# A vector spread over the partitions by TensorE instead of by a DMA, and one column of the first modulation made by sixteen one-column matmuls

## The chip, the cores and the metric

One core of a Trainium2 chip. Its engines each run their own instructions in order and wait for each other by semaphores: TensorE (PE; PEld is its weight load), VectorE (DVE), ScalarE (ACT), GpSimd (POOL) and SyncE (SP), which here issues all DMAs. The metric is device time in microseconds, median of several runs. Times below count from the start of the profiled span.

## The reference

Two layers on x of 256 tokens by 2048 channels, all float32. Layer 0 is a Mamba-2 mixer, layer 1 a dilated window attention. Each layer modulates its input by a conditioning vector c, and only this matters here:

```
shift, scale, gate = split(silu(c) @ ada_w[layer] + ada_b[layer], 3)
h = x * (1.0 + scale) + shift
proj = h @ a_in_w            # layer 0: 2048 -> 10304 columns
```

So shift and scale of layer 0, 2048 numbers each, must be there before the first big product starts, 128 channels (one tile kt of 16) at a time.

## The kernel before

**Big products.** Activations lie channel by token (tile kt is 128 channels by 256 tokens). Every float32 operand of a big product is split into a high part (a copy on ScalarE, rounded to the float32r type) and a low part (a subtraction on VectorE), and three float32r matmuls make one product. A weight "piece" is 128 x 1024 floats, 0.52 MB, and holds two tiles kt by 512 columns. It comes by DMA into `raw` (6 buffers, `load_piece`, L87-90), is split by `split` (L92-99) into `whi` (L95, ScalarE) and `wlo` (L97, VectorE), 4 buffers each, and is used either by `cm_piece` (24 matmuls of 256 columns, L121-123) or by `tm_piece` (12 matmuls of 512 columns, L169-171).

**The modulation.** silu(c) lies in `cb_`, the same 2048 numbers on every partition: a DMA that reads c 128 times (`bcast`, L67) and a SiLU on ScalarE (L68). A column (128 values of shift or scale) is made by `ada_load` (a DMA of 1.05 MB, `araw<-in_ada`, L240) and `ada_dot` (one VectorE multiply with running sum over 128 x 2048, L247). `ada_bias` (L252) adds the bias row. Then `h_step` (L381-400) makes tile kt of h: htmp (L397, ScalarE), its high part actT (L398, ScalarE) and its low part (L399, VectorE).

**Stage one**, up to about 180 us, interleaves the 32 columns of layer 0 with the pieces. A hand-written list, `order`, gives the order of the pieces; its first entries are z/B/C pieces b4:0, b6:0, h (first piece of B/C group 0), z2:0, b2:0, x1:0. In front of the loop stand the first DMAs, all on SP's queue: c, columns scale 0 and shift 0, x, the bias, pieces 0 and 1, scale 1, piece 2. Each `h_step` fetches another column, and each turn of the loop one more piece, so that five pieces are fetched ahead of the one in use. PE works on a tile kt as soon as its h is there. A scheduler places each engine's instructions in order of its own estimate, so that a change in one place can move instructions in another.

**Stage two**, from about 180 us, computes dt and the scan of each head group: `stage1` (seg, L567-570; xd and the like, L580-588, VectorE) and `stage2` (py, L608, PE, float32; po, L600), with the remaining pieces in between. L351 and L358 add a stored part of a product to its rest.

Of the kernel before, what the change touches and what calls it, by code (L numbers as in the profile page):

```python
# [9 lines left out]
F32 = mybir.dt.float32  # L10
F32R = mybir.dt.float32r
I32 = mybir.dt.int32
AF = mybir.ActivationFunctionType
ALU = mybir.AluOpType
# [4 lines left out]
P = 128  # L19
L = 256  # L20
D = 2048
KT = D // P
# [24 lines left out]


@with_exitstack
def trunk(ctx, tc, xT, x, c, par, cst, bias, lnrow, ada, wdt, win, wout, wk, wv, wbin, wbout, out):  # L50
    nc = tc.nc
    V, S, T, PO = nc.vector, nc.scalar, nc.tensor, nc.gpsimd

    cons = ctx.enter_context(tc.tile_pool(name="cons", bufs=1))
    wp = ctx.enter_context(tc.tile_pool(name="wp", bufs=3))
# [3 lines left out]
    mm = ctx.enter_context(tc.tile_pool(name="mm", bufs=4, space=PSUM))  # L59
    aux = None  # L60

    def bcast(dst, src, off=0):
        nc.sync.dma_start(dst, bass.AP(tensor=src.tensor, offset=src.offset + off,
                                       ap=[[0, P], [1, dst.shape[-1]]]))

    cb_ = cons.tile([P, D], F32, name="cb_")
    bcast(cb_, c)  # L67
    S.activation(cb_, cb_, AF.Silu)  # L68
    NB = OFF["adab"][1]
    adab_ = cons.tile([P, NB], F32, name="adab")  # L70
    prm = cons.tile([P, NPAR - NB], F32, name="prm")
    cc = cons.tile([P, NCONST], F32, name="cc")

    cons.tile([P, 32], F32, name="pad")

    def pv(name):
        a, b = OFF[name]
# [4 lines left out]
    cbmask = cc[:, CM:CM + 384]  # L82
    ones = cons.tile([P, P], F32, name="ones")
    V.memset(ones, 1.0)


    def load_piece(src):  # L87
# [86 lines left out]
    def tm_pair():  # L174
        return [mm.tile([P, 512], F32, name="acc") for _ in range(2)]
# [52 lines left out]
    mod = [cons.tile([P, KT, 3], F32, name=f"mod{i}") for i in range(2)]  # L228
# [3 lines left out]
    def shift(i, kt):  # L232
        return mod[i][:, kt, 0:1]

    def scale(i, kt):
        return mod[i][:, kt, 1:2]

    def ada_load(pool, layer, kind, ct):
        raw = pool.tile([P, D], F32, name="araw", bufs=2)
        nc.sync.dma_start(raw, ada[layer, KIND.index(kind), ct])  # L240
        return raw

    def ada_dot(layer, kind, ct, raw):

        j = KIND.index(kind)
        with tc.issue_after(pin[0]) if pin[0] is not None else ExitStack():
            V.scalar_tensor_tensor(raw, raw, 1.0, cb_, op0=ALU.mult, op1=ALU.mult,  # L247
                                   accum_out=mod[layer][:, ct, j:j + 1])

    def ada_bias(layer, kts, kinds):  # L250
        m = mod[layer][:, kts, kinds]
        V.tensor_tensor(m, m, adab[:, layer, kts, kinds], op=ALU.add)  # L252
# [33 lines left out]
    with ExitStack() as cA:  # L286
# [14 lines left out]
        with ExitStack() as cS:  # L301
            wp1 = cS.enter_context(tc.tile_pool(name="wp1", bufs=2))
# [62 lines left out]
            with ExitStack() as c0:  # L365
# [1 line left out]
                ex = c0.enter_context(tc.tile_pool(name="ex", bufs=4, space=PSUM))  # L367
                first = [acc_pair(ex), acc_pair(ex)]
                cols = [(0, kind, kt) for kt in range(KT) for kind in ("scale", "shift")]
                raws, xts, late = [], {}, []  # L370

                def fetch():
                    i = len(raws)
                    if i < len(cols):
                        raws.append(ada_load((wp1, pe)[i // 2 % 2], *cols[i]))

                def fetch_x(kt):
                    xts[kt // 2] = pe.tile([P, 2, L], F32, name="xt")
                    nc.sync.dma_start(xts[kt // 2], xT[:, kt:kt + 2, :])

                def h_step():  # L381

                    _, kind, kt = cols[h_step.i]
                    raw = raws[h_step.i]
                    h_step.i += 1
                    if kind == "scale" and kt % 2 == 0 and kt:
                        fetch_x(kt)
                    ada_dot(0, kind, kt, raw)
                    if kt > 1:
                        pin[0] = None  # L390
                    fetch()
                    while late:
                        late.pop()()
                    if kind == "shift":
                        ada_bias(0, slice(kt, kt + 1), slice(0, 2))
                        t = pe.tile([P, L], F32, name="htmp")
                        S.activation(t, xts[kt // 2][:, kt % 2, :], AF.Identity, bias=shift(0, kt), scale=scale(0, kt))  # L397
                        S.activation(hhi[:, kt, :], t, AF.Copy)  # L398
                        late.append(lambda: V.tensor_tensor(hlo[:, kt, :], t, hhi[:, kt, :].bitcast(F32),  # L399
                                                            op=ALU.subtract))  # L400
# [7 lines left out]
                for row in ("b4:0. b6:0. h z2:0. b2:0 x1:0 h", "b2:1. x1:1. z1:0 z1:1. z4:0 h h",  # L408
# [3 lines left out]
                    for w in row.split():  # L412
                        if w == two:
                            n = -2 if sum(o[0] == -2 for o in order) == sum(o[0] == -1 for o in order) else -1
# [6 lines left out]
                pieces = []  # L421

                def fetch_piece():
                    if len(pieces) < len(order):
                        k, q, _ = order[len(pieces)]
                        pieces.append(load_piece(source[k][q]))

                fetch()
                fetch()
                fetch_x(0)  # L430
                nc.sync.dma_start(adab_, par[:, :NB])
                V.tensor_scalar(adab[:, :, :, 1:3], adab[:, :, :, 1:3], 1.0, None, op0=ALU.add)
                fetch_piece()
                fetch_piece()
                fetch()
                fetch_piece()
                for _ in range(2):
                    for _ in range(2):
                        h_step()
                    while late:  # L440
                        pin[0] = late.pop()().ins
                    fetch_piece()

                def dt_piece(q, raw):
# [26 lines left out]
                            else:  # L471
                                S.activation(place, ps[w], AF.Copy)

                begin, done, ended, halves = {}, set(), [], {}
                for i, (k, q, ends) in enumerate(order):
                    fetch_piece()
                    if i == 16:
# [236 lines left out]
        for n in range(4):  # L714
            ps = tm_chunk(wout[n], lambda kt: yhi[kt // 16][:, kt % 16, :], lambda kt: ylo[kt // 4][:, kt % 4, :],
                          nk=2 * KT, rate=(1, 4) if n else (0, 1),
                          pre={0: y_ahead, 3: first_weights}.get(n), split_end=4 if n == 3 else 0)
# [45 lines left out]
    with ExitStack() as cL:  # L763
# [25 lines left out]
        with tc.issue_after(tile4.ins):  # L789
# [12 lines left out]
            late = latest[-1].ins  # L802
# [123 lines left out]
    for n in range(2):  # L926
        ps = tm_chunk(wbout[n], *og, nk=H)
# [12 lines left out]
    ps = [tm_pair() for _ in range(2)]  # L940
# [19 lines left out]
    halves = [ps[1], [None, aux2.tile([P, 512], F32, name="po")]]  # L960
# [31 lines left out]
def _cm(v):  # L992

    return v.reshape(-1, P).T
# [9 lines left out]
def _dt(w):  # L1004

    a = np.zeros((2, 8, P, P), w.dtype)
    a[..., :64] = w.reshape(2, 8, P, 64)
    return a.transpose(0, 2, 1, 3).reshape(2, P, 1024)


def _layout(x, c, ada_w, ada_b, ln_g, ln_b, a_in_w, a_conv_w, a_conv_b, a_dt_bias,
            a_A_log, a_D, a_norm_g, a_out_w, kv_w, b_in_w, b_out_w):
    f = np.float32
    par = np.zeros((P, NPAR), f)

    def put(name, a):
        par[:a.shape[0], OFF[name][0]:OFF[name][1]] = a

    ab = ada_b.reshape(2, 3, KT, P)
    put("adab", ab.transpose(3, 0, 2, 1).reshape(P, 96))  # L1020
    put("convw", a_conv_w[0].T.reshape(48, P, 4).transpose(1, 0, 2).reshape(P, 192))
    put("convb", _cm(a_conv_b[0]))
    put("normg", _cm(a_norm_g[0]))
    put("dsk", np.broadcast_to(a_D[0], (P, 64)))
    put("dtb", a_dt_bias[0][:, None])
    put("alog", np.broadcast_to(a_A_log[0], (P, 64)))
    put("lng", _cm(ln_g[0]))
    put("lnb", _cm(ln_b[0]))

    cst = np.zeros((P, NCONST), f)  # L1030
    i = np.arange(P)
    cst[:, CI:CI + 128] = np.eye(P)
    up = (i[:, None] <= i[None, :]).astype(f)
    cst[:, CT:CT + 128] = up
    cst[:, CM:CM + 384] = np.concatenate([up, up, np.ones((P, P), f)], 1)
    bias = np.zeros((P, NBIAS), f)
    delta = 128 + i[:, None] - np.arange(256)[None, :]
    bias[:, CD:CD + 256] = -delta
    for g, (win_, dil) in enumerate(((128, 1), (512, 4), (2048, 16))):
        ok = (delta >= 0) & (delta % dil == 0) & (delta <= win_)  # L1040
        bias[:, CA + 256 * g:CA + 256 * g + 256] = np.where(ok, 0.0, NEG)


    ada = ada_w.reshape(2, D, 3, KT, P).transpose(0, 2, 3, 4, 1)

    w = a_in_w[0]
    z, xs, bb, cc, dt = (w[:, a:b] for a, b in ((0, 4096), (4096, 8192), (8192, 9216), (9216, 10240), (10240, 10304)))
    bc = np.stack([bb.reshape(D, G, P), cc.reshape(D, G, P)], 2).reshape(D, 2048)
    win = _pieces(np.concatenate([bc, xs, z], 1))
    return {  # L1050
        "xT": x[0].T.reshape(KT, P, L).transpose(1, 0, 2), "x": x[0], "c": c, "par": par, "cst": cst, "bias": bias,
        "lnrow": np.stack([ln_g[0], ln_b[0], ln_g[1], ln_b[1]]),
        "ada": ada, "wdt": _dt(dt), "win": win,
        "wout": _pieces(a_out_w[0]), "wk": _pieces(kv_w[:, :3072], 256, 4),
        "wv": _pieces(kv_w[:, 3072:]), "wbin": _pieces(b_in_w[0], 256, 4), "wbout": _pieces(b_out_w[0]),
    }
# [20 lines left out]
```

## Time and profile before

| | |
|---|---|
| median of 3 runs | 1275.31 us (1274.89 to 1276.96) |
| profiled execution, device time | 1274.67 us |
| its span in the trace | 1272.5 us |
| PE busy | 1236.6 us, 97% |
| DVE busy | 1034.5 us, 81% |
| ACT busy | 704.0 us, 55% |
| DMA queue q1 | 334.69 MB, 73.5% of 16 engines' span |
| first matmul | 15.01 us |

A row of the timeline gives start, duration, engine, source line, operation, the tile written and read, and in brackets the idle time ahead of it with what ended it. "L" numbers are lines of the kernel before, unless a row is said to be of the changed kernel, whose lines are some 26 (around the splits) to 41 (in stage two) higher.

### The profile page before, as it was taken

The numbers are of one execution on the slowest core, as the hardware profiler recorded it, in microseconds if no ns is written. First come the engines' busy times: TensorE is split into PE (matmuls) and PEld (weight loads), VectorE is DVE, ScalarE is ACT, GpSimd is POOL, SyncE is SP. The second block draws the span as 40 slices with busy tenths as digits, with TensorE's granted clock in tenths as the row PEclk, the third lists the DMA queues.
The fourth block names the chain that finished last, engine by engine and source line by source line (L and its number), as shares of the span: only waits on it lengthen the run. The fifth ranks groups of instructions, "written<-read, shape, count | busy, mean of one in ns | idle before, by whom it ended". The sixth has DMA issues, their size and how long they took to land.

```text
span 1272.5 us, 19056 instructions
## 1 busy us (share of the span) xinstructions
PE 1236.6 (97%) x7222; PEld 1078.7 (85%) x7222; DVE 1034.5 (81%) x1498; ACT 704.0 (55%) x1035; POOL 0.2 (0%) x4
## 2 busy tenths in 40 slices
PE   4999999999999999999999999999999999999997
PEld 4889989899898999778888788888878888888885
DVE  6999986999998878869776678878888867758876
ACT  3655577757677777764344445434345645444731
POOL 0000000000000000000000000000000000000000
PEclk9999999999999999999999999999999999999999
DMA  9999968696866546468988469989998774463751
GB/s 386 423 420 422 420 211 298 224 341 234 314 247 208 157 149 216 167 216 292 338 282 282 160 195 353 357 328 348 357 381 316 235 240 130 127 204 100 222 192 66
DMA packets 80588, 335.89 MB, mean 264 GB/s; under 512 B 9105, under 2 KB 9329, under 8 KB 67697
## 3 DMA queue, kind: packets, MB, share of 16 engines
q1 hardware_dynamic: 80496, 334.69, 73.5%
q8 instruction: 56, 0.92, 0.3%
q14 instruction: 36, 0.29, 0.1%
HBM read 332.47 MB, written 2.18 MB: 263 GB/s over the span
## 4 chain that ended last, share of the span: by engine, by line
PE 85%; DVE 8%; DMA 3%; issue 2%; ACT 1%; SPq 0%; DVEq 0%; ACTq 0%
PE acc L145 14%; PE acc L171 12%; PE acc L170 12%; PE acc L169 12%; PE acc L148 7%; PE acc L123 7%; PE acc L121 7%; PE acc L122 7%; DVE araw L247 2%; DVE wlo L97 2%; PE py L608 2%; PE aux L850 1%; DMA araw<-in_ada 1%; DMA raw<-in_wk 1%; PE po L873 1%
## 5 line engine op out<-in xcount | busy, mean ns | idle before, releaser
L95 ACT ACTIVATE whi<-raw 128x1024 fp32r<-128x1024 f32 x392 | 411.3, 1058 | 369.4 <-PE acc L171 127.3
L97 DVE TENSOR_TENSOR wlo<-raw,whi 128x1024 fp32r<-128x1024 f32 x392 | 473.3, 1220 | 140.3 <-ACT whi L95 139.5
L145 PE MATMUL acc<-actT,whi 128*128 128x512 f32 x896 | 285.9, 398 | 0.0
L170 PE MATMUL acc<-wlo,actT 128*128 128x512 f32 x688 | 269.7, 392 | 1.1 <-DVE wlo L97 0.9
L169 PE MATMUL acc<-whi,actT 128*128 128x512 f32 x688 | 266.7, 394 | 0.9 <-ACT actT L663 0.9
L121 PE MATMUL acc<-actT,whi 128*128 128x256 f32 x768 | 217.4, 285 | 17.5 <-ACT actT L398 17.3
L247 DVE SCALAR_TENSOR_TENSOR araw<-araw,cb__72 128x2048 f32<-128x2048 f32 x96 | 219.2, 2284 | 14.6 <-DMA araw<-in_ada 14.5
L123 PE MATMUL acc<-actT,wlo 128*128 128x256 f32 x768 | 214.9, 285 | 4.9 <-DVE wlo L97 4.9
L122 PE MATMUL acc<-actT,whi 128*128 128x256 f32 x768 | 217.1, 284 | 0.0
L148 PEld LDWEIGHTS acc<-actT,wlo 128*128 128x128 f32 x896 | 167.0, 188 | 42.1 <-DVE wlo L97 5.0
L148 PE MATMUL acc<-actT,wlo 128*128 128x256 f32 x896 | 180.9, 282 | 1.9 <-DVE wlo L97 1.2
L171 PE MATMUL acc<-whi,actT 128*128 128x512 f32 x432 | 168.7, 391 | 0.0
L121 PEld LDWEIGHTS acc<-actT,whi 128*128 128x128 f32 x768 | 147.7, 193 | 18.7 <-ACT actT L398 17.5
L170 PEld LDWEIGHTS acc<-wlo,actT 128*128 128x128 f32 x688 | 129.3, 188 | 29.1 <-DVE wlo L97 3.4
L123 PEld LDWEIGHTS acc<-actT,wlo 128*128 128x128 f32 x768 | 146.5, 193 | 6.0 <-DVE wlo L97 5.8
L169 PEld LDWEIGHTS acc<-whi,actT 128*128 128x128 f32 x688 | 128.7, 188 | 26.7 <-ACT actT L663 1.4
L122 PEld LDWEIGHTS acc<-actT,whi 128*128 128x128 f32 x768 | 148.1, 193 | 0.3
L145 PEld LDWEIGHTS acc<-actT,whi 128*128 128x128 f32 x896 | 137.5, 189 | 0.3
L171 PE MATMUL acc<-whi,ylo 128*128 128x512 f32 x256 | 100.5, 393 | 0.0
L171 PEld LDWEIGHTS acc<-whi,actT 128*128 128x128 f32 x432 | 81.1, 188 | 16.6
L171 PEld LDWEIGHTS acc<-whi,ylo 128*128 128x128 f32 x256 | 48.0, 188 | 9.7
L319 DVE SCALAR_TENSOR_TENSOR cacc<-acc,prm,cacc 128x253 f32<-128x253 f32 (+2 forms) x96 | 42.1, 474 | 6.1 <-ACT cacc L316 5.8
(251 smaller groups left out, 1110.2 us busy)
## 6 DMA issues: line engine op xcount, KB each, us to landing
araw<-in_ada SPq DMA_DIRECT2D x96, 1024.0 KB, 7.5
raw<-in_win SPq DMA_DIRECT2D x160, 512.0 KB, 5.6
raw<-in_wout SPq DMA_DIRECT2D x64, 512.0 KB, 4.8
raw<-in_wbin SPq DMA_DIRECT2D x64, 512.0 KB, 4.3
raw<-in_wv SPq DMA_DIRECT2D x48, 512.0 KB, 5.4
raw<-in_wk SPq DMA_DIRECT2D x48, 512.0 KB, 7.7
cbc<-cumd SPq DMA_DIRECT2D x16, 512.0 KB, 5.2
raw<-in_wbout SPq DMA_DIRECT2D x16, 512.0 KB, 4.7
```

The costliest lines, as they stand in the source:

```text
L95: copied.append(S.activation(hi, raw, AF.Copy))
L97: latest.append(V.tensor_tensor(lo, raw, hi.bitcast(F32), op=ALU.subtract))
L121: T.matmul(o, hi[:, k, c_], ahi[:, kt, :], start=first, stop=False, skip_group_check=True)
L122: T.matmul(o, hi[:, k, c_], alo[:, kt, :], start=False, stop=False, skip_group_check=True)
L123: T.matmul(o, lo[:, k, c_], ahi[:, kt, :], start=False, stop=kt == k1 - 1, skip_group_check=True)
L145: T.matmul(ps[n], hi[:, k, n * P:n * P + P], xp[:, kt], start=kt == 0, stop=False, skip_group_check=True)
L148: T.matmul(ps[n][:, 0, :], lo[:, k, n * P:n * P + P], xhi[:, kt, :], start=False, stop=kt == KT - 1, skip_group_check=True)
L169: T.matmul(o, h_, hi[:, k, :], start=kt == k0, stop=False, skip_group_check=part)
L170: T.matmul(o, h_, lo[:, k, :], start=False, stop=False, skip_group_check=part)
L171: end = T.matmul(o, l_, hi[:, k, :], start=False, stop=kt == k1 - 1, skip_group_check=part)
L247: V.scalar_tensor_tensor(raw, raw, 1.0, cb_, op0=ALU.mult, op1=ALU.mult, accum_out=mod[layer][:, ct, j:j + 1])
L319: V.scalar_tensor_tensor(acc[:, o:], ps[:, :L - o], w[:, j:j + 1], acc[:, o:], op0=ALU.mult, op1=ALU.add)
```

## The change

1. **c.** The DMA of c into all partitions goes. The host now lays c out as 128 x 528: columns 0 to 511 hold the four quarters of c, quarter j on partitions 32j to 32j+31, and columns 512 to 527 hold c by rows (channel 128k+p at partition p, column k). `spread_c` loads it, applies SiLU, keeps the last 16 columns as `ccol`, splits the 512 others into high and low, and multiplies them by 0/1 matrices `pick` (made by GpSimd memsets) in eight matmuls of 512 columns. Four PSUM banks are copied to `cb_`, two by ScalarE, two by VectorE.
2. **First shift column.** Fetch number 1 loads `adak` (the same 1.05 MB of weights, laid out so that channels stand on the partitions). Its dot product on VectorE becomes sixteen float32 matmuls with one moving column each (`raw` block k as weights, `ccol[:, k]` moving), and a copy of 128 values from PSUM.
3. **Order at the start.** Piece 0 is split ahead of the first `h_step`, piece 1 after the first tile, and one `fetch_piece` less stands ahead of the loop, so that four pieces are fetched ahead instead of five.

```diff
-    bcast(cb_, c)
-    S.activation(cb_, cb_, AF.Silu)
+    def spread_c():
+        cq = wp.tile([P, 1024], F32, name="raw", bufs=6)[:, :512 + KT]
+        nc.sync.dma_start(cq, c)
+        pick = wp.tile([P, 1024], F32R, name="whi", bufs=4)[:, :512].rearrange("p (j m) -> p j m", j=4)
+        PO.memset(pick.bitcast(F32), 0.0)
+        for j in range(4):
+            PO.memset(pick[32 * j:32 * j + 1, j, :].bitcast(F32), 1.0)
+        S.activation(cq, cq, AF.Silu)
+        V.tensor_copy(ccol, cq[:, 512:])
+        half = wp.tile([P, 1024], F32R, name="wlo", bufs=4).rearrange("p (i n) -> p i n", i=2)
+        S.activation(half[:, 0, :], cq[:, :512], AF.Copy)
+        V.tensor_tensor(half[:, 1, :], cq[:, :512], half[:, 0, :].bitcast(F32), op=ALU.subtract)
+        ps = [mm.tile([P, 512], F32, name="acc") for _ in range(4)]
+        for js in ((0, 1), (2,), (3,)):
+            for i in range(2):
+                for j in js:
+                    T.matmul(ps[j], pick[:, j, :], half[:, i, :], start=i == 0, stop=i == 1)
+        for j in range(4):
+            d = cb_[:, 512 * j:512 * j + 512]
+            if j % 2:
+                V.tensor_copy(d, ps[j])
+            else:
+                S.activation(d, ps[j], AF.Copy)
...
                 def fetch():
                     i = len(raws)
-                    if i < len(cols):
+                    if i == 1:
+                        raws.append(wp1.tile([P, D], F32, name="araw", bufs=2))
+                        nc.sync.dma_start(raws[1], adak)
+                    elif i < len(cols):
...
-                    ada_dot(0, kind, kt, raw)
+                    if h_step.i == 2:
+                        pm = mm.tile([P, 2, L], F32, name="acc")[:, 0, 0:1]
+                        for k in range(KT):
+                            T.matmul(pm, raw[:, k * P:k * P + P], ccol[:, k:k + 1], start=k == 0, stop=k == KT - 1)
+                        with tc.issue_after(dot[0]):
+                            V.tensor_copy(mod[0][:, 0, 0:1], pm)
+                    else:
+                        dot[0] = ada_dot(0, kind, kt, raw).ins
...
+                halves = {}
+                spread_c()
                 fetch()
                 fetch()
                 fetch_x(0)
...
                 fetch_piece()
-                fetch_piece()
                 fetch()
                 fetch_piece()
-                for _ in range(2):
-                    for _ in range(2):
-                        h_step()
+                halves[0] = split(pieces[0])
+                for i in range(2):
+                    h_step()
+                    h_step()
                     while late:
                         pin[0] = late.pop()().ins
+                    if i == 0:
+                        halves[1] = split(pieces[1])
                     fetch_piece()
```

**At the start, on VectorE.** Below is the head of VectorE's program, after two memsets: before, then changed. `mod` holds the columns, `araw` the weights of a column, `adab` the bias.

```order
L247 SCALAR_TENSOR_TENSOR araw,mod_84<-araw,cb__72 128x2048 x2
L432 TENSOR_SCALAR adab<-adab 128x32x2
L252 TENSOR_TENSOR mod_84<-mod_84,adab 128x2
L97 TENSOR_TENSOR wlo<-raw,whi 128x1024
L399 TENSOR_TENSOR actT<-htmp,actT 128x256
L97 TENSOR_TENSOR wlo<-raw,whi 128x1024
L247 SCALAR_TENSOR_TENSOR araw,mod_84<-araw,cb__72 128x2048
L97 TENSOR_TENSOR wlo<-raw,whi 128x1024
L247 SCALAR_TENSOR_TENSOR araw,mod_84<-araw,cb__72 128x2048
L252 TENSOR_TENSOR mod_84<-mod_84,adab 128x2
```

```order
L107 COPY cb__72<-acc_141 128x512 [waits PE_49]
L273 SCALAR_TENSOR_TENSOR araw_154,mod0_83<-araw_154,cb__72 128x2048 [waits DMAHW1_49,DVE_49,Activation_49]
L471 TENSOR_SCALAR adab_73<-adab_73 128x32x2 [waits DMAHW4_49]
L423 COPY mod0_83<-acc_175 128x1 [waits PE_49]
L278 TENSOR_TENSOR mod0_83<-mod0_83,adab_73 128x2 [waits DVE_49]
L123 TENSOR_TENSOR wlo_169<-raw_162,whi_168 128x1024 [waits DMAHW5_49,Activation_49]
L436 TENSOR_TENSOR actT_87<-htmp_196,actT_87 128x256 [waits Activation_49]
L273 SCALAR_TENSOR_TENSOR araw_164,mod0_83<-araw_164,cb__72 128x2048 [waits DMAHW6_49]
L123 TENSOR_TENSOR wlo_201<-raw_166,whi_200 128x1024 [waits DMAHW7_49,Activation_49]
L273 SCALAR_TENSOR_TENSOR araw_173,mod0_83<-araw_173,cb__72 128x2048 [waits DMAHW0_49]
L278 TENSOR_TENSOR mod0_83<-mod0_83,adab_73 128x2 [waits DVE_49]
```

The second dot (L247) became a copy that waits for PE (L423), and two splits of pieces instead of three stand ahead of the second bias.

**In stage two, on VectorE**, around the first head group (`s` is y of the group, `xd` its input times dt): before, then changed.

```order
L97 TENSOR_TENSOR wlo<-raw,whi 128x1024 x6
L358 TENSOR_TENSOR s_95<-acc,s_95 128x512 x2
L557 TENSOR_TENSOR cb<-aux,cc 128x384
...
L580 TENSOR_TENSOR xd<-aux,dtT 128x512
L583 TENSOR_TENSOR s_95<-aux,prm 128x512
L97 TENSOR_TENSOR wlo<-raw,whi 128x1024 x3
L601 TENSOR_TENSOR xo<-aux,dec 128x512
```

```order
L123 TENSOR_TENSOR wlo<-raw,whi 128x1024 x5
L384 TENSOR_TENSOR s_94<-acc,s_94 128x512 x2
L598 TENSOR_TENSOR cb<-aux,cc 128x384
...
L621 TENSOR_TENSOR xd<-aux,dtT 128x512
L624 TENSOR_TENSOR s_94<-aux,prm 128x512
L123 TENSOR_TENSOR wlo<-raw,whi 128x1024 x4
L642 TENSOR_TENSOR xo<-aux,dec 128x512
```

One split of a piece moved from ahead of the group to behind it.

**In stage two, on PE**, at the same group (`py` is its product, `acc` a big product): before, then changed.

```order
L169 MATMUL acc<-whi,actT 128x512 x2
L608 MATMUL py<-xd,seg 128x64 x8
L121 MATMUL acc<-actT,whi 128x256
L600 MATMUL aux<-xo,cb 128x512
L608 MATMUL py<-xd,seg 128x64 x8
L122 MATMUL acc<-actT,whi 128x256
```

```order
L195 MATMUL acc<-whi,actT 128x512 x2
L649 MATMUL py<-xd,seg 128x64 x8
L641 MATMUL aux<-xo,cb 128x512
L649 MATMUL py<-xd,seg 128x64 x8
L595 MATMUL aux<-bcm 128x2x128
L596 MATMUL aux<-bcm 128x128
```

Between the transposes ahead of them (L578, changed L619) and the first py, PE has 32 matmuls of 512 columns before and 20 in the changed kernel; the other 12, one piece, come behind the py.

More of the change, by code (lines that the diff above doesn't have):

```diff
@@ L49, in trunk @@
 @with_exitstack
-def trunk(ctx, tc, xT, x, c, par, cst, bias, lnrow, ada, wdt, win, wout, wk, wv, wbin, wbout, out):
+def trunk(ctx, tc, xT, x, c, par, cst, bias, lnrow, ada, adak, wdt, win, wout, wk, wv, wbin, wbout, out):
     nc = tc.nc
@@ L72, in trunk @@
     cc = cons.tile([P, NCONST], F32, name="cc")
-    cons.tile([P, 32], F32, name="pad")
+    cons.tile([P, 16], F32, name="pad")
     def pv(name):
@@ L84, in trunk @@
     V.memset(ones, 1.0)
+    ccol = cons.tile([P, KT], F32, name="ccol")
+    def spread_c():
[21 more added lines that the diff above has]
+                S.activation(d, ps[j], AF.Copy)
     def load_piece(src):
@@ L246, in ada_dot @@
         with tc.issue_after(pin[0]) if pin[0] is not None else ExitStack():
-            V.scalar_tensor_tensor(raw, raw, 1.0, cb_, op0=ALU.mult, op1=ALU.mult,
-                                   accum_out=mod[layer][:, ct, j:j + 1])
+            return V.scalar_tensor_tensor(raw, raw, 1.0, cb_, op0=ALU.mult, op1=ALU.mult,
+                                          accum_out=mod[layer][:, ct, j:j + 1])
     def ada_bias(layer, kts, kinds):
@@ L369, in trunk @@
                 cols = [(0, kind, kt) for kt in range(KT) for kind in ("scale", "shift")]
-                raws, xts, late = [], {}, []
+                raws, xts, late, dot = [], {}, [], [None]
                 def fetch():
                     i = len(raws)
-                    if i < len(cols):
+                    if i == 1:
+                        raws.append(wp1.tile([P, D], F32, name="araw", bufs=2))
+                        nc.sync.dma_start(raws[1], adak)
+                    elif i < len(cols):
                         raws.append(ada_load((wp1, pe)[i // 2 % 2], *cols[i]))
@@ L472, in put_away @@
                                 S.activation(place, ps[w], AF.Copy)
-                begin, done, ended, halves = {}, set(), [], {}
+                begin, done, ended = {}, set(), []
                 for i, (k, q, ends) in enumerate(order):
@@ L1044, in _layout @@
     ada = ada_w.reshape(2, D, 3, KT, P).transpose(0, 2, 3, 4, 1)
+    adak = ada_w[0, :, :P].reshape(KT, P, P).transpose(1, 0, 2).reshape(P, D)
+    crow = np.concatenate([np.repeat(np.reshape(c, (4, 512)), 32, 0), np.reshape(c, (KT, P)).T], 1)
     w = a_in_w[0]
@@ L1050, in _layout @@
     return {
-        "xT": x[0].T.reshape(KT, P, L).transpose(1, 0, 2), "x": x[0], "c": c, "par": par, "cst": cst, "bias": bias,
+        "xT": x[0].T.reshape(KT, P, L).transpose(1, 0, 2), "x": x[0], "c": crow, "par": par, "cst": cst, "bias": bias,
         "lnrow": np.stack([ln_g[0], ln_b[0], ln_g[1], ln_b[1]]),
-        "ada": ada, "wdt": _dt(dt), "win": win,
+        "ada": ada, "adak": adak, "wdt": _dt(dt), "win": win,
         "wout": _pieces(a_out_w[0]), "wk": _pieces(kv_w[:, :3072], 256, 4),
```

## Prediction

> **What bounds the kernel now.** I read the page's slices first, then what PE waited for, then the busy time by stretches, then the first 40 us engine by engine.
>
> ```profile
> PE   4999999999999999999999999999999999999997
> DVE  6999986999998878869776678878888867758876
> DMA  9999968696866546468988469989998774463751
> PE acc L121 <- ACT actT L398: 17.3, 2, 15.0
> PE acc L123 <- DVE wlo L97: 4.9, 4, 1.9
> 40.00:60.00 20.00, 20.00 (x137) 18.57 (x136) 18.62 (x20) 12.94 (x18) 0.00 (x0) 1.00 1.02 421
> 140.00:160.00 20.00, 20.00 (x159) 19.51 (x158) 19.27 (x21) 10.68 (x14) 0.00 (x0) 1.00 1.00 412
> ```
>
> PE is full but for the first slice. Its largest wait by far is for the first h: 15.0 us once, 2.3 us for the second tile. In the stretches (columns: PE, PEld, DVE, ACT, POOL busy, clock, DMA share, GB/s) PE is full from 40 us, but DVE has 18.6 to 19.3 of 20 us and the DMA moves 0.42 MB/us without a pause. So what the start saves arrives at the end only if none of the three is late, and what another order costs later is not hidden.
>
> The start is a chain:
>
> ```profile
> 5.58 1.91 ACT L68 ACTIVATE cb__72<-cb__72 128x2048 f32<-128x2048 f32 x1 [3.58 <-DMA cb__72<-in_c]
> 8.10 2.29 DVE L247 SCALAR_TENSOR_TENSOR araw<-araw,cb__72 128x2048 f32<-128x2048 f32 x1 [7.10 <-DMA araw<-in_ada]
> 10.47 2.29 DVE L247 SCALAR_TENSOR_TENSOR araw<-araw,cb__72 128x2048 f32<-128x2048 f32 x1
> 12.91 0.16 DVE L252 TENSOR_TENSOR mod<-mod,adab 128x2 f32<-128x2 f32 x1
> 13.11 0.60 ACT L397 ACTIVATE htmp<-xt,mod 128x256 f32<-128x256 f32 x1 [5.62 <-DVE mod L252]
> 13.61 1.04 ACT L95 ACTIVATE whi<-raw 128x1024 fp32r<-128x1024 f32 x1
> 14.56 0.40 ACT L398 ACTIVATE actT<-htmp 128x256 fp32r<-128x256 f32 x1
> ```
>
> c lands at 5.6, the first column at 8.05, two dots end at 12.7, the bias at 13.07. A copy of piece 0 stands between htmp and actT, and PE starts at 15.01. SiLU of c is hidden under the first column's DMA.
>
> **The change at the start.** Spreading c:
>
> ```profile
> L472 ACT ACTIVATE s<-acc 128x512 f32<-128x512 f32 x16 | 8.9, 594 | 5.0 <-PE acc L123 2.4 <-PE acc L171 2.3
> L679 DVE TENSOR_TENSOR u<-acc,gt 128x512 f32<-128x512 f32 x8 | 5.2, 683 | 4.2 <-PE acc L171 4.2
> 17.11 0.41 PE L122 MATMUL acc<-actT,whi 128*128 128x256 f32 x1
> 17.32 0.41 PE L123 MATMUL acc<-actT,wlo 128*128 128x256 f32 x1
> 19.74 0.28 PE L123 MATMUL acc<-actT,wlo 128*128 128x256 f32 x1
> 19.86 0.28 PE L121 MATMUL acc<-actT,whi 128*128 128x256 f32 x1
> ```
>
> c is 128 x 528 x 4 bytes, 0.27 MB, not 1.05; 0.78 MB less at 0.42 MB/us is 1.9 us, so it lands at 3.7. SiLU and high part at 0.6 us each (L472, same width): 4.9. Eight matmuls of 512 columns: PE's first matmuls stand 0.21 us apart at 256 columns, from 19.2 us on 0.12, so I take 0.42: done at 8.3. The last of four evictions on DVE (0.7, as L679): `cb_` at 9.0 to 9.2. The scale dot then ends at 11.5 and the bias addition at 11.6. POOL's memsets are not in the trace; by DVE's memset of 128x128 (0.17 us, in its first microsecond) they take 1 to 2 us and have until 4.9, so I cost them at nothing; were they late, the whole chain would be.
>
> The shift column: `adak` is the third DMA, 2.37 MB into the stream, where the first column before was at 2.10 MB and landed at 8.05: 8.7. Then sixteen float32 matmuls, of a kind with
>
> ```profile
> L608 PE MATMUL py<-xd,seg 128*128 128x64 f32 x256 | 29.9, 272 | 0.0
> 229.08 1.89 PE L608 MATMUL py<-xd,seg 128*128 128x64 f32 x16
> 230.78 0.37 PE L121 MATMUL acc<-actT,whi 128*128 128x256 f32 x1
> ```
>
> The program has 128 py matmuls and the trace 256: a float32 matmul is two passes. Eight took 1.70 us (229.08 to 230.78), 0.21 each, and since 64 columns cost as much there as a weight load, one column won't be cheaper: sixteen take 3.4 us at full clock. That is the lower end. At the early clock (0.21 against 0.12 above, up to twice) 6.0 to 6.8 us is the upper end. Before, the clock rose 4.2 us after the first matmul (15.01 to 19.2); from 4.9 that is 9.1, which would give 3.6 us. But one moving column per weight load keeps the array mostly empty. I take 4.4 us, nearer the low end: column at 13.1.
>
> The Trainium skill ("TensorE: Matmul & The Clock Gate", Part 1) says that TensorE runs at half clock until it was busy for about 3.4 us on end, within a window that runs freely. The trace's 4.2 us agrees. By that rule the eight spreading matmuls, 3.4 us, fill one window only by luck: by the rule taken strictly this term is 6.8 us, by the row 3.6.
>
> Copy and bias add 0.3: both columns stand at 13.4, against 13.07 before. **The start gains nothing in the columns**: one dot less on DVE, but it starts a microsecond later, and PE's sixteen matmuls end behind it. What it gains is that piece 0 has been split on ACT before, so htmp and actT (0.60 and 0.40) follow directly: PE starts at 14.5, 0.5 sooner.
>
> From there DVE decides. Its rows before:
>
> ```profile
> 14.69 1.23 DVE L97 TENSOR_TENSOR wlo<-raw,whi 128x1024 fp32r<-128x1024 f32 x1 [1.61 <-ACT whi L95]
> 15.83 0.42 DVE L399 TENSOR_TENSOR actT<-htmp,actT 128x256 fp32r<-128x256 f32 x1
> 33.00 3.49 DVE L97 TENSOR_TENSOR wlo<-raw,whi 128x1024 fp32r<-128x1024 f32 x3
> 24.29 0.74 PE L121 MATMUL acc<-actT,whi 128*128 128x256 f32 x4 [2.30 <-ACT actT L398]
> 34.28 0.39 PE L123 MATMUL acc<-actT,wlo 128*128 128x256 f32 x1 [1.92 <-DVE wlo L97]
> ```
>
> With 2.2 for a dot, 1.15 for a split, 0.35 for a low part: split 13.4, low part to 15.0, scale 1 to 17.2, split to 18.4, shift 1 to 20.6, bias 20.8, then ACT; second tile on PE at 21.9 (before 24.29, but with one piece less done ahead of it). Low part 22.3, scale 2 24.5, split 25.7, shift 2 27.9, bias, scale 3 30.4, split of piece 3 at 31.6. The columns are there in time (shift 1 lands at 5.8 MB, 16.9 us; scale 3 at 9.5 MB, 25.7). PE, which waits for that split, then has 10 matmuls of 512 columns (0.23 each) and 4 of 256 to the point where it stood at 34.28 before: 31.7 + 2.3 + 0.5 = 34.5. **The offset is +0.2 us**, namely the time of the sixteen matmuls less 4.2: between -0.8 and +2.6. From there to 180 us PE is full and carries it.
>
> SP's queue: fetch of scale 2 waits for the sixteen matmuls (same buffer), and piece 2, shift 2 and scale 3 stand behind it. At 13.1 scale 1, piece 1 and shift 1, to 16.9 us, are still in flight; a DMA takes about 2.35 us before its data flow (c: 0.73 to 5.58 less 2.5 of transfer), so nothing is lost unless the matmuls end after 14.6, and then up to 1 us. One piece less fetched ahead is free as long as DVE and not the DMA is last; pieces come 0.3 us later to 1.9 sooner than before. I take 0; bounds 0 and 1 us.
>
> **The change in stage two.** The order moved there, too:
>
> ```profile
> 217.21 2.36 DVE L97 TENSOR_TENSOR wlo<-raw,whi 128x1024 fp32r<-128x1024 f32 x2 [0.67 <-ACT whi L95]
> 227.37 0.68 DVE L580 TENSOR_TENSOR xd<-aux,dtT 128x512 f32<-128x512 f32 x1
> 231.15 3.48 DVE L97 TENSOR_TENSOR wlo<-raw,whi 128x1024 fp32r<-128x1024 f32 x3
> 241.68 1.37 DVE L351 TENSOR_TENSOR sz<-acc,sz 128x512 f32<-128x512 f32 x2
> 245.32 1.22 DVE L97 TENSOR_TENSOR wlo<-raw,whi 128x1024 fp32r<-128x1024 f32 x1
> 246.59 0.39 PE L123 MATMUL acc<-actT,wlo 128*128 128x256 f32 x1 [0.73 <-DVE wlo L97]
> 206.23 1.57 ACT L567 ACTIVATE seg<-cbc,cumT 128x128 f32<-128x128 f32 x5
> ```
>
> DVE has no pause here after the 0.67 us at 217.21, and PE waits for it at 246.59. PE begins py at 229.08, one microsecond after xd (228.05). In the changed kernel 12 matmuls of 512 columns, 2.75 us, stand behind py instead of ahead: PE would be there at 226.3. xd comes about 0.4 sooner (a split of 1.15 moved behind the group, but ACT runs one seg instead of five ahead of a copy that waits for its buffer, and its next copies are about 0.8 late): PE waits some 1.4 to 1.8 us. The 12 matmuls then end the product 1.5 us later, L351 waits for it, and behind L351 stand a dot and the split for which PE waits at 246.59. PE had 0.73 us of slack there, but DVE is what is late. I cost it at +1.6; ends: 0 (the wait falls where PE would have waited anyway) and 2.75 (all twelve). Behind it the same order is executed, with PE full.
>
> Sum: +0.2 + 1.6 = **+1.8 us** on the profiled execution's own 1274.67: 1276.5. The median of the runs is 0.64 above that execution, so I say **1277.1**; own range 1275.5 to 1278.6 (matmuls 3.6 to 5.5, stage two 0.8 to 2.0).
>
> **Rivals.**
> - *Slow clock.* The sixteen matmuls run at the early clock all through, from 8.7 to 15.5: offset +2.6, queue included, sum +4.2, 1279.5: slower than before. For it: 3.4 us of work ahead of them against 4.2 before the rise at 15 us. Against: PE never stops for more than 0.4 us between 4.9 and their end. It decides at 5.2 us for the sixteen (sum above 2.55).
> - *Stage two costs nothing*, since PE's wait for xd replaces that at 246.59, and the clock rises at 9.1: -0.6, 1274.7. For it: the 0.73 there. Against: DVE without a pause.
> - *Starved.* Four pieces ahead are too few in a stretch with DMA and DVE both near full: +0.8 more, 1277.9. For it: the DMA share of 1.0. Against: pieces wait on DVE's slots as it is.
> - *No use of the early c:* it lands at 3.7, but nothing depends on it; that is within the forecast.
>
> **How the numbers follow.** Forecast 0.55, slow clock 0.2, free stage two 0.15, starved 0.1. The range 1274.3 to 1279.8 takes in all four and leaves out their far ends. 0.2%, 2.55 us, is about what can be told from no change here: slower beyond 1277.86 has most of the slow clock, half of the starved case and a tenth of the forecast, 0.3; faster below 1272.76 needs what no term gives, 0.05; within, 0.65.
>
> **What would show it.** c's SiLU at 3.7; the eight matmuls from 4.9; the sixteen from 8.7, and their end; the first bias (before 12.91) near 13.2; PE's first big matmul at 14.5 and its last early wait ending near 31.7; a new PE wait of 1.4 to 1.8 us ahead of py near 227. I am wrong if the sixteen take under 3 us, if PE has no wait ahead of py, or if new waits for DMA appear between 40 and 160 us.

## The result, and the profile after

The changed kernel takes **1282.85 us** (median of 6 runs, 1281.38 to 1285.03) against 1275.8 before (6 runs, 1274.77 to 1277.07): ratio 1.0053, 95% interval 1.0043 to 1.0063, so 7 us slower. The forecast was 1277.1 us with a range of 1274.3 to 1279.8. The profiled execution took 1283.97 us; its span is 1282.2, that is 9.7 more than before. Two executions ran in a slow state, one of e1 below (2498.84 us) and one of the kernel before beside e12 (1639.39 us); the ratios leave them out, the medians 1282.35 and 1275.95 count them.

The page's slices: PEclk (the clock that TensorE was granted, in tenths of full speed) before, then PE and PEclk of the changed kernel:

```profile
PEclk9999999999999999999999999999999999999999
PE   6999999999999999999999999999999999999997
PEclk8999999899999999999999999999999999999999
```

PE looks as full as before. What is new is in PEclk: below full speed in the first slice and in the eighth, 224 to 256 us. PE's waits in the changed kernel (in total, times, longest):

```profile
PE acc L147 <- ACT actT L435: 3.6, 2, 2.1
PE acc L149 <- DVE wlo L123: 3.6, 4, 1.6
PE aux L619 <- DVE cb L598: 2.0, 2, 1.4
PE py L649 <- DVE xd L621: 1.6, 1, 1.6
```

The single wait of 15 us for the first h is gone, since PE works from 4.97 us on. The one ahead of py is there, and for cb PE waits twice, 1.4 us at most, ahead of the transposes (L619, before L578). The start, row by row:

```profile
3.52 0.64 ACT L94 ACTIVATE raw<-raw 128x528 f32<-128x528 f32 x1 [1.50 <-DMA raw<-in_c]
4.97 3.69 PE L103 MATMUL acc<-wlo,whi 128*128 128x512 f32 x8 [4.97 <-ACT wlo L97]
8.78 4.16 PE L421 MATMUL acc<-ccol,araw 128*128 128x1 f32 x32
13.17 0.16 DVE L278 TENSOR_TENSOR mod<-mod,adab 128x2 f32<-128x2 f32 x1
14.47 0.80 PE L147 MATMUL acc<-actT,whi 128*128 128x256 f32 x2 [1.53 <-ACT actT L435]
21.76 0.97 PE L147 MATMUL acc<-actT,whi 128*128 128x256 f32 x4 [2.10 <-ACT actT L435]
31.32 0.50 PE L196 MATMUL acc<-wlo,actT 128*128 128x512 f32 x1 [0.55 <-DVE wlo L123]
```

To follow the loss, two marks that both kernels pass serve below: **A**, PE's first product of a head group (`aux<-bcm`), before at 218.70, and **B**, the wait for a low part some 28 us on, before at 246.59 (quoted in the prediction). Stage two around them, before and then changed:

```profile
199.10 0.51 SPq L546 DMA_DIRECT2D cumd<-araw  x1
202.32 0.81 SPq L562 DMA_DIRECT2D cbc<-cumd  x2
203.24 7.13 SPq L89 DMA_DIRECT2D raw<-in_win  x4
214.24 1.04 ACT L95 ACTIVATE whi<-raw 128x1024 fp32r<-128x1024 f32 x1
215.31 1.23 DVE L97 TENSOR_TENSOR wlo<-raw,whi 128x1024 fp32r<-128x1024 f32 x1 [5.30 <-ACT whi L95]
218.70 0.60 PE L554 MATMUL aux<-bcm 128*128 128x256 f32 x2
```

```profile
201.37 0.34 SPq L115 DMA_DIRECT2D raw<-in_win  x1
202.50 0.81 SPq L603 DMA_DIRECT2D cbc<-cumd  x2
208.88 0.40 ACT L608 ACTIVATE seg<-cbc,cumT 128x128 f32<-128x128 f32 x1 [2.64 <-DMA cbc<-cumd]
216.89 1.04 ACT L121 ACTIVATE whi<-raw 128x1024 fp32r<-128x1024 f32 x1
217.97 1.23 DVE L123 TENSOR_TENSOR wlo<-raw,whi 128x1024 fp32r<-128x1024 f32 x1 [6.48 <-ACT whi L121]
218.79 0.60 PE L595 MATMUL aux<-bcm 128*128 128x256 f32 x2
222.81 0.65 PE L619 MATMUL aux<-cc,xs 128*128 128x128 f32 x4 [1.36 <-DVE cb L598]
228.88 0.68 DVE L621 TENSOR_TENSOR xd<-aux,dtT 128x512 f32<-128x512 f32 x1
229.62 3.07 PE L649 MATMUL py<-xd,seg 128*128 128x64 f32 x16 [1.58 <-DVE xd L621]
254.59 0.39 PE L149 MATMUL acc<-actT,wlo 128*128 128x256 f32 x1 [0.48 <-DVE wlo L123]
```

Mark A is 0.09 us late, mark B 8.00: **in this execution 7.9 of the 9.7 us are lost within 28 us, and nothing at the start.** (Another 1.1 us are gone at the next wait for a low part: PE's matmul of 255.07 before stands at 264.05, and 9.07 late behind it.) Read the rows as a chain. `cbc` is the load from which ScalarE makes seg. In the changed kernel a weight piece (201.37) stands ahead of it on SP; ScalarE waits 2.64 us for cbc and makes its seg at 208.88, not at 206.23; the copies queued behind are late by as much (216.89, before 214.24), VectorE's low part waits for them (217.97, before 215.31), and behind it come cb, for which PE waits 1.36 us, and xd, for which it waits 1.58.

The rest is the clock. Stretches of the changed kernel (columns: PE busy, granted clock, DMA share, GB/s):

```profile
226.89:230.30 3.41, 1.83 (x12) 1.00 0.00 0
230.30:240.54 10.24, 10.24 (x38) 0.50 0.49 150
25.50:230.30 204.80, 199.85 (x1320) 1.00 0.90 351
```

From 25.50 to 230.30 us the clock is full, then at half for 10.24 us, and sixteen py records take 3.07 us where they took 1.89. Half speed for 10.24 us costs 5.1. From A to B: 1.36 + 1.58 + 5.12, less 0.25 (the wait at B is 0.48, not 0.73), is 7.8 of the 7.9. That is this one execution; e11 below, a second one of the same kernel, loses 2.6 us at the start and 3.0 between the marks.

### The profile page after: what moved, and what is told of

Its sections match the earlier page's. It is cut to its first block, busy times and chain, and to the rows that moved or that the text cites. A ratio compares the mean times of both kernels' runs of the same rounds, so it can differ in the third digit from the quotient of the medians.

```text
span 1282.2 us, 19152 instructions
## 1 busy us (share of the span) xinstructions
PE 1251.4 (98%) x7262; PEld 1090.9 (85%) x7262; DVE 1035.9 (81%) x1501; ACT 702.8 (55%) x1036; POOL 1.5 (0%) x9
## 3 DMA queue, kind: packets, MB, share of 16 engines
HBM read 331.69 MB, written 2.18 MB: 260 GB/s over the span
## 4 chain that ended last, share of the span: by engine, by line
PE 84%; DVE 9%; DMA 4%; issue 2%; ACT 2%; DVEq 0%; SPq 0%; ACTq 0%
PE acc L171 14%; PE acc L196 12%; PE acc L197 12%; PE acc L195 12%; PE acc L174 7%; PE acc L149 6%; PE acc L147 6%; PE acc L148 6%; DVE araw L273 2%; PE py L649 2%; DVE wlo L123 2%; PE aux L891 1%; DMA araw<-in_ada 1%; PE po L914 1%; DVE cacc L345 1%
```

## The experiments

Theory A: what costs the time is the order in stage two, set by the number of pieces fetched ahead. Theory B: the start costs it. The offset at some time is how much later PE stands at the same matmul than in the profile before. Each median stands beside that of the kernel before on the same chip, and ratios carry their 95% interval.

**e1, four pieces ahead, alone.** In the kernel before:

```diff
                 fetch_piece()
-                fetch_piece()
                 fetch()
                 fetch_piece()
```

> The kernel before with one fetch_piece less ahead of the loop, nothing else: c by DMA, both first columns by VectorE. Its stage-two order (from the dt step on) is then that of the changed kernel, instruction by instruction. Theory A (the order in stage two costs the time, and the number of pieces fetched ahead sets that order): 6 to 9 us over the kernel before, with PE waits of about 1.4 us ahead of the transposes and 1.6 us ahead of the first py, and the granted clock at half for one to three stretches of 3.4 us behind them. Theory B (the spreading and the sixteen matmuls at the start cost it): within 0.5 us of the kernel before.

1282.35 against 1276.21, ratio 1.0042 (1.0027 to 1.0057). ScalarE waits 2.03 us for cbc, PE 1.58 ahead of py, and the clock is at half for 6.83 us: mark B is 7.72 late, mark A 1.75 (of which 1.50 are there at 40 us). One line that has nothing to do with c does what the whole change does.

**e2, the changed kernel with the fifth piece.** The line removed above goes back in.

> The changed kernel with the fifth piece fetched ahead again: spreading, sixteen matmuls and early splits stay. Its stage-two order is that of the kernel before. Theory A: all of the loss goes; the offset at the start was -0.18 us in the profiled execution, so 1274.5 to 1276, no new wait ahead of py, clock 1.0 from 26 us on. Theory B: still some 1282 us.

1276.53 against 1276.21, ratio 0.9999 (0.9989 to 1.0009). With e1 this settles it between the theories: with five pieces ahead the spreading and the sixteen matmuls cost nothing that can be measured, and gain nothing. In its profile:

```profile
8.85 6.96 PE L421 MATMUL acc<-ccol,araw 128*128 128x1 f32 x32
17.33 0.79 PE L147 MATMUL acc<-actT,whi 128*128 128x256 f32 x2 [1.53 <-ACT actT L435]
208.21 1.57 ACT L609 ACTIVATE seg<-cbc,cumT 128x128 f32<-128x128 f32 x5 [0.59 <-DMA cbc<-cumd]
249.23 0.39 PE L149 MATMUL acc<-actT,wlo 128*128 128x256 f32 x1 [0.73 <-DVE wlo L123]
```

The sixteen matmuls took 6.96 us here, since the clock rose only at 21.2; the start is 1.47 us late in this execution, where it was 0.18 early in the changed kernel's. And some wait for cbc (0.59, and 0.55 for the second) is there even in the order of before.

**e3, work put into the wait.** In `stage2`, ahead of the first py of the first group:

```diff
                     py = aux2.tile([P, 512], F32, name="py")
+                    if g == 0 and b == 0:
+                        flat = segs[1].rearrange("p h b n -> p (h b n)")
+                        for n in (512, 256):
+                            T.matmul(py[:, :n], ident, flat[:, :n], start=True, stop=True)
```

> The changed kernel with two float32 matmuls more (512 and 256 columns, the identity times the second seg tile) directly ahead of the first py of the first head group; py overwrites their result. They start when seg is there, at about 228.2, and end at about 229.6, where PE waited idle for xd. If the idle time makes the clock fall (theory A with the clock): no stretch at half clock behind 230 us, py back to 1.9 us for sixteen records, and 3 to 5 us less than the changed kernel: 1278 to 1280. If the clock fell for another reason, or the order alone costs the time: no gain, or 0.2 us more.

1281.48, ratio 1.0045 (1.0030 to 1.0060): not to be told from the changed kernel's 1.0053. In the profile the filler lies where the wait was, and the clock stays full:

```profile
227.63 1.56 PE L650 MATMUL py<-seg,cc 128*128 128x512 f32 x4 [0.18 <-DVE seg L611]
225.00:240.00 15.00, 14.74 (x78) 1.00 0.35 109
```

That is one execution, which also waited for cbc only 1.45 us; the gain of 3 to 5 us was not reached in the median. Inconclusive.

**e4, the first shift column by VectorE again** (`if h_step.i == 2` and `if i == 1` never true), four pieces ahead.

> The changed kernel with the first shift column made by VectorE again (from the usual weights), spreading and early splits kept, four pieces ahead. Stage-two order as in the changed kernel. VectorE then has a dot of 2.3 us where it waited 1.1 and copied: the first bias about 0.9 us later (14.1 instead of 13.2), and with VectorE full to 31 us the offset rises from -0.2 to about +0.7 us at 100 us. Theory A: 1282 to 1285, since the stage-two order stays. Theory B: back near 1276.

1282.76, ratio 1.0054 (1.0035 to 1.0073): theory A's value. ScalarE waits 2.30 us for cbc, PE 1.02 and 1.57, and the clock does not fall behind 228 us. PE's first big matmul is at 16.74 and the offset at 100 us is 2.1, not 0.7: VectorE's order here puts a split ahead of the first bias, which was not foreseen.

**e5 and e6, cbc of the first group from GpSimd's queue**, with four and with five pieces ahead:

```diff
-                    nc.sync.dma_start(cbc, ...)
+                    (nc.gpsimd if g == 0 else nc.sync).dma_start(cbc, ...)
```

> The changed kernel (four pieces ahead), in which the two cbc loads of the first head group are issued from GpSimd's queue, which is idle, not from SP's, where a piece stands ahead of them. In the changed kernel ScalarE waited 2.64 us for cbc at 208.9. Its order else stays, but for one xd (ahead of the conv instead of behind it) and the seg instructions beside a copy or two. If that queue place is what makes cb and xd late: ScalarE waits under 0.7 us for cbc, PE waits under 0.5 us ahead of the transposes and of the first py, no clock at half behind 228 us, 1276 to 1279 us. If the twelve matmuls that stand behind py are the cause by themselves: a wait of 1 us or more ahead of py stays, and 1281 to 1284 us.

> The changed kernel with five pieces ahead again (as in e2) and the same two cbc loads on GpSimd's queue; order on PE, VectorE and ScalarE as in e2. There ScalarE waited 0.59 and 0.55 us for cbc and PE then 1.1 us ahead of the transposes. If that wait goes: 0.5 to 1.1 us less than e2, 1275.2 to 1276.2. If GpSimd issues these loads more slowly than SP: the same as e2 or up to 2 us more.

Both misses: 1286.07, ratio 1.0071 (1.0059 to 1.0083), and 1282.41, ratio 1.0053 (1.0041 to 1.0065). Meant to bring cbc earlier, the edit brought it later: 8.3 us from issue to landing from GpSimd's queue in e6, against 5.7 for the same two loads from SP's in e2. That the queue itself is slower isn't shown: SP no longer held its own loads behind cbc, and issued a column of 1.05 MB at 203.04 and the first of four pieces at 203.47, just ahead. But e6 has, on PE, VectorE and ScalarE, the very order of e2. Its rows:

```profile
203.56 1.19 POOL L604 DMA_DIRECT2D cbc<-cumd  x2 [201.28 <-DMA cumd<-araw]
210.88 1.57 ACT L609 ACTIVATE seg<-cbc,cumT 128x128 f32<-128x128 f32 x5 [4.55 <-DMA cbc<-cumd]
225.94 1.12 PE L620 MATMUL aux<-cc,xs 128*128 128x128 f32 x4 [3.29 <-DVE cb L599]
253.56 0.39 PE L149 MATMUL acc<-actT,wlo 128*128 128x256 f32 x1 [0.74 <-DVE wlo L123]
224.13:230.96 6.83, 5.02 (x14) 0.50 0.48 165
```

A late cbc makes the whole loss without the twelve matmuls that moved behind py: the start is 0.20 us late, mark B 6.97, and the clock is at half for 6.83 us. So the changed order on PE isn't needed for the loss: e2 and e6 differ in which queue issues cbc, and so in when it lands, and theory A is narrowed to the landing of cbc.

**e7 and e8, matmuls ahead of the spreading**, five pieces ahead; e8 has e6's edit too:

```diff
+        V.memset(cb_[:, :512], 1.0)
+        for _ in range(2):
+            T.matmul(ps[0], ones, cb_[:, :512], start=True, stop=True)
         for js in ((0, 1), (2,), (3,)):
```

> e2 with two float32 matmuls of 512 columns (ones times ones) on PE ahead of the eight spreading matmuls, from about 1.6 to 5 us, where PE was idle; the spreading overwrites their result. In e2 the clock rose only at 21.2 us and the sixteen one-column matmuls took 6.96 us; in the changed kernel it rose at 8.4 and they took 4.16. If the clock rises with a stretch of 3.4 us that is full of matmuls: it is at full by 8.5 in every execution, the sixteen take 3.4 to 4.2 us, PE's first big matmul is at 13.9 to 14.6 and the offset to the kernel before at 100 us is -0.2 to -0.6: 0.3 to 1.5 us less than e2. If the clock does not follow from PE's work ahead: as e2.

> e6 and e7 together: five pieces ahead, the two matmuls ahead of the spreading, cbc of the first group on GpSimd's queue. If both gains hold and add: 1274 to 1275.5, so that it is some 1 us under the kernel before. If neither holds: 1276 to 1278.

e7: 1276.43, ratio 1.0009 (1.0000 to 1.0018); e8: 1284.52, ratio 1.0069 (1.0056 to 1.0082), e6's loss again. Rows of e7, then the sixteen in e8:

```profile
5.02 2.21 PE L106 MATMUL acc<-wlo,whi 128*128 128x512 f32 x8
8.84 4.01 PE L424 MATMUL acc<-ccol,araw 128*128 128x1 f32 x32 [1.61 <-DMA araw<-in_adak]
15.32 0.58 PE L150 MATMUL acc<-actT,whi 128*128 128x256 f32 x1 [2.47 <-ACT whi L124]
8.82 6.05 PE L424 MATMUL acc<-ccol,araw 128*128 128x1 f32 x32 [0.98 <-DMA araw<-in_adak]
```

In e7 the eight matmuls take 2.21 us instead of 3.69 and the sixteen 4.01, as expected, but PE's first big matmul stands at 15.32, since it now waits for a copy on ScalarE. In e8, with the same two matmuls ahead, the clock falls at 9.81 and the sixteen take 6.05 us; its start is 3.77 us late, the most of all. So full speed for the sixteen in every execution, which was expected, is a miss, and nothing is gained in the median.

**e9, cbc first on SP**, four pieces ahead. The pieces of the next product get an edge behind the group's second cbc load:

```diff
+        with tc.issue_after(cbc_last[0]) if cbc_last[0] is not None else ExitStack():
+            nc.sync.dma_start(raw, src)
-        nc.sync.dma_start(raw, src)
...
+                    if g == 0:
+                        cbc_last[0] = last.ins
```

> The changed kernel (four pieces ahead), with one edge more on SP's queue: the pieces of the product behind the first head group are issued behind that group's cbc loads, not ahead of them. On PE, VectorE and ScalarE its order is that of e5, instruction by instruction, where cbc came from GpSimd's queue and ScalarE waited 6.4 us for it. If the landing of cbc decides: ScalarE waits under 0.7 us for it, PE waits under 0.5 us ahead of the transposes and of py, no clock at half near 228, 1275 to 1278 us, some 8 us under e5 in the same order. If the order with four pieces ahead costs by itself: a PE wait of over 1 us stays, 1280 to 1283 us.

1278.45 against 1276.81, ratio 1.0017 (1.0004 to 1.0029).

```profile
204.11 0.82 SPq L606 DMA_DIRECT2D cbc<-cumd  x2
209.10 1.26 ACT L613 ACTIVATE seg<-cbc,cumT 128x128 f32<-128x128 f32 x4
231.71 1.10 PE L646 MATMUL aux<-xo,cb 128*128 128x512 f32 x2 [0.57 <-DVE xo L634]
250.06 0.39 PE L152 MATMUL acc<-actT,wlo 128*128 128x256 f32 x1 [0.48 <-DVE wlo L126]
```

ScalarE doesn't wait for cbc, PE waits 0.57 us once between A and B, the clock is full. In the same order on PE, VectorE and ScalarE as e5, without e5's 6.39 us of waiting for cbc, it stands at 1.0017 of the kernel before instead of 1.0071.

**e10 and e11, e1 and the changed kernel once more** (e10's label names an edge that this kernel doesn't have).

> e1 once more, for a second profile of it on this chip: the granted clock's stretches lie on a grid of 3.41 us that starts elsewhere in each execution, so the stretch at half clock behind the wait ahead of py is 0, 3.4, 6.8 or 10.2 us long (6.8 in e1), and the time between 1278 and 1284 us.

> The changed kernel again, for its time beside e9 on one chip and a second profile: 1281 to 1285 us, ScalarE waiting over 2 us for cbc at 208 to 211, PE over 1 us ahead of the first py; the half clock behind it between 0 and 10.2 us by the place of the 3.41 us grid.

e10, one run: 1279.81, cbc wait 0.80, PE 1.39 ahead of py, 3.41 us at half clock. e11: 1284.43 against 1276.81, ratio 1.0055 (1.0040 to 1.0071), measured on e9's chip and 6 us above it. Its profiled execution:

```profile
211.33 0.40 ACT L608 ACTIVATE seg<-cbc,cumT 128x128 f32<-128x128 f32 x1 [2.39 <-DMA cbc<-cumd]
232.06 2.00 PE L649 MATMUL py<-xd,seg 128*128 128x64 f32 x16 [1.60 <-DVE xd L621]
228.29:231.70 3.41, 2.18 (x10) 1.00 0.00 0
```

The same wait ahead of py, 1.60 us, and no fall of the clock behind it: from A to B it loses 3.0 us, where the first execution of the same program lost 7.9. Its start, on the other hand, is 2.56 us late at 40 us, where the first was 0.18 early: here the sixteen matmuls took 6.96 us.

**e12, e1 with e9's edge.**

> e1 (the kernel before with four pieces ahead) with the edge of e9: the pieces of the next product behind the first group's cbc loads on SP. No spreading, no sixteen matmuls. e9 stayed 2 us over the kernel before, its profile 2.8 us late at the start and only 0.7 us in stage two. If that rest is the start: this one is within 1 us of the kernel before, and 4 to 6 us under e1. If it is the order with four pieces ahead: 1.5 to 2.5 us over the kernel before, as e9.

1277.70 against 1275.95, ratio 1.0013 (1.0002 to 1.0023), where e1 had 1.0042. So most of e1's loss goes with the edge, and the rest of e9 isn't owed to the changed start: with the start of before it is as large. In the profiles of e1, e10 and e12 the offset is 1.50, 1.53 and 1.58 at 40 us already, so the missing fetch costs some 1.5 us at the start of the kernel before, besides what it does in stage two.

The profiles side by side, from mark A to mark B (27.89 us before). The fourth column is PE's busy time at half clock behind A, the last the loss less half of it, an estimate of what would be lost at full clock:

| kernel | ScalarE's wait for cbc | A to B, more than before | PE busy at half clock | loss without the clock |
|---|---|---|---|---|
| before | 0 | 0 | 0 | 0 |
| e7, e9, e12 | 0 | -0.15, 0.42, 0.41 | 0 | -0.2 to 0.4 |
| e10 | 0.80 | 2.88 | 3.41 | 1.2 |
| e2 | 1.14 | 1.17 | 0 | 1.2 |
| e3 (filler) | 1.45 | 2.06 | 0 | 2.1 |
| e1 | 2.03 | 5.97 | 6.83 | 2.6 |
| e4 | 2.30 | 2.94 | 0 | 2.9 |
| e11 | 2.39 | 3.04 | 0 | 3.0 |
| changed | 2.64 | 7.91 | 10.24 | 2.8 |
| e8 | 4.27 | 6.93 | 5.86 | 4.0 |
| e6 | 4.55 | 6.79 | 5.02 | 4.3 |
| e5 | 6.39 | 7.87 | 4.70 | 5.5 |

The last column follows the first to within 0.9 us, whatever the start and whatever the order on PE: what ScalarE waits for cbc comes out at PE. No version beats the kernel before; e2 equals it.

## Why the prediction was wrong

1. **The start was right**, in the profiled execution to within 0.4 us: c 3.52 (3.7), the eight matmuls from 4.97 (4.9) to 8.66 (8.3), the sixteen from 8.78 (8.7) to 12.94 (13.1), both columns 13.3 (13.4), PE 14.47 (14.5), second tile 21.76 (21.9), last early wait 31.32 (31.7), offset -0.18 (+0.2). That the columns gain nothing held, too: 13.3 against 13.07 before, and e2 is at 0.9999. In e11, the same kernel once more, the offset is 2.56, so part of this agreement is luck, as the next point shows.
2. **The 4.4 us of the sixteen met an early rise of the clock.** The seven profiles that have this start as it stands show 3.85 to 4.68 us in four (4.16 in the first) and 6.96 in three (e2, e9, e11), which is the rival of the slow clock; the offset at 40 us ran from -0.2 to 2.8 us in them. The bounds, -0.8 and +2.6, nearly held that, and e2's median doesn't show it.
3. **The wrong step was the one that costed stage two at +1.6**, in its sentence "xd comes about 0.4 sooner". xd ended at 229.56, before at 228.05: 1.5 later. The step weighed the instructions on PE, VectorE and ScalarE, and left out SP's queue there, on which a piece had moved ahead of cbc. It read ScalarE's five seg instructions that became one as a gain for the copies, and didn't ask whether cbc would be there for that one: ScalarE waited 2.64 us for it. The sum closes with that: 2.65 late at the copy of 216.89, less the split of 1.15 that had moved, is the 1.5 of xd. In place of +1.6 the marks A and B show a loss of 7.9 us in the first profile and 3.0 in e11. The wait ahead of py (1.58, forecast 1.4 to 1.8) came out right only because PE itself was 1.36 us late by then.
4. **The second part of that step was the clock.** The prediction priced it for the start and not for a wait in the middle: 0 in e11 to 5.1 us in the first profile, for the same wait of 1.6. The step's ends, 0 and 2.75 for all twelve matmuls, were bounds of the wrong mechanism.
5. **"One piece less fetched ahead is free"** was right as it was meant, no piece was late: between 40 and 180 us the offset stands at -0.18 without a change. It was wrong as a sum, because that line is what reorders stage two: with it e1, without it e2. The prediction took the two for separate edits. And in the kernel before the same line costs 1.5 us at the start (e1, e10, e12); why, no run here shows.

What stays open: why ScalarE waits 1.5 to 2.6 us for cbc in most executions behind one piece, where 0.52 MB at 0.42 MB/us are 1.25 (and 0.8 in e10); how the median's 7 us divide between start, wait and clock, since e3 didn't settle it and the profiles show only single executions; and how much of the 1.7 us of e9 and e12 is the start, where e12's profile has 1.6 us, with 0.4 between A and B.

## What to carry to other kernels

Where a scheduler places the instructions, an edit at the head can reorder what comes 200 us later, and the DMA queue is part of that order: look for a load with short slack that a bulk load has overtaken. Undo a change line by line before pricing its purpose; here two kernels of one line each (e1, e2) did more than any sum. And a wait of PE can cost more than its length: half clock behind one of 1.6 us added from nothing to 5.1 us here.

## What the runs showed of the hardware

- **The clock changes on a grid of 3.41 us**, whose place differs from execution to execution. In the changed kernel:

```profile
8.44:11.85 3.41, 3.29 (x29) 1.00 0.96 355
11.85:18.68 6.83, 5.30 (x24) 0.50 1.01 425
18.68:22.09 3.41, 1.31 (x10) 1.00 1.01 423
22.09:25.50 3.41, 3.41 (x18) 0.50 1.01 424
```

  Every stretch is one, two or three times 3.41 us (the 204.8 above are 60 times). Ahead of a trace's first change the column reads 1.00 though the matmuls run at the early clock, so there the spacing has to be read.
- **PE busy isn't what counts.** From 8.44 to 11.85 PE was busy 3.29 us, nearly all of it one-column matmuls, and the clock fell; 1.83 us with py in them (226.89) let it fall; 2.18 us of 512-column matmuls (e11, 228.29) did not. What counts instead isn't shown. Behind the fall ahead of py the clock stayed at half for 3.4 (e10) to 10.2 us (changed kernel), and PE's being busy didn't raise it: in the changed kernel PE was busy all through 233.72 to 237.13, most of it with py, and the clock stayed at half. The Trainium skill ("TensorE: Matmul & The Clock Gate", Part 1) has the clock fall after an idle stretch of about 3.4 us; the trace's grid agrees with that length, but here a stretch with a wait of 1.6 us was enough, so the measurement decides.
- **Sixteen float32 matmuls with one column** are 32 records in the trace. They took 3.85 us in e6, nearly all of it at full clock, and 6.96 in e2, all at half: some 0.11 and 0.22 us a record. The 64-column py took 0.11 at full clock as well.
- **Moving a load to another queue didn't bring it sooner:** cbc from GpSimd's queue took 8.3 us to land in e6, the same loads from SP's 5.7 in e2; SP's own loads ran beside them in e6, so the queue alone isn't priced by this.
